# Twenty-six input projections as two-by-two block products with seven multiplications, in a hybrid decoder block

## The chip, the cores and the metric

The kernel runs on one core of one Trainium2 chip. The metric is the device time of one execution in microseconds (us). The engines are TensorE (PE in the rows), VectorE (DVE), ScalarE (ACT), GpSimd (POOL) and SyncE (SP), which here issues nearly all transfers.

## The reference

One decoder block, T = D = 1024, in float32:

```
h  = RMSNorm(x)
P  = h @ W_in        columns for retention, SSD, GLA heads and merge gates
a  = retention (4 heads), b = Mamba-2 SSD (16 heads, conv, 2 groups), c = GLA (4 heads)
x  = x + (sig(g_a)*a + sig(g_b)*b + sig(g_c)*c) @ W_out
x  = x + relu(RMSNorm(x) @ W_up)^2 @ W_down
out = final RMSNorm(x)
```

## The kernel before

Every large product is done in float32r parts: `split` takes an operand apart into hi (a cast on ACT) and lo (a subtraction on DVE), and `acc3` adds hi·hi, hi·lo and lo·hi in PSUM, three matmuls per 128 rows of depth. A weight comes by one SP transfer into `raw` and is split into `whi` and `wlo`.

W_in is cut into 34 sets of 256 columns. In channel form (`T_unit`) a set is four units of 24 matmuls of 128x512, with weights as the stationary operand and h as the moving one, so results have channels on the partitions. In token form (`tok_unit`) a unit is 24 matmuls of 128x256 (128x288 for the first set) for one block of 128 tokens. Two sets for retention's v and two for GLA's v were in token form. `x` came transposed from the host; 1/rms per token was applied to the products, by `rs_b` in DVE's reading of PSUM and by a scale in ACT's.

`stream` yields after each unit. `merge(main, nmain, mixer, nmix)` deals the steps of a mixer evenly over `nmain` units, in program order, which is the order on every engine's own queue. Retention and the first group of the SSD's projections ran together, then SSD group 0 with the projections of group 1, SSD group 1 with GLA's projections, and GLA (`gla_mixer`, 18 steps, two per chunk and two head pairs) with 28 of the 48 gate units. The other 20 were run by `gates_done`, called behind `load_o(0)`, which loads the first token half of the 16 mixer output tiles (`oraw`), scales them and splits them into `ohi` and `olo`. Then `branch_half(0)` multiplies these with `w_o`, and the output projection, the MLP and the last norm follow:

```
    merge(stream(g_jobs()), 32, ssd_mixer(1), 26)
...
    merge(itertools.islice(gates, 28), 28, gla_mixer(), 18)
...
    for _ in load_o(0, o):
        pass
    gates_done()
```

`finish_heads` squares each head's output on ACT (`hsq`), takes the power on POOL (`rs_r`), scales (`og`), transposes on TensorE, multiplies by the gate (`ot`) and stores. In GLA, ACT makes the decays (`kx`, `ge`), DVE the decayed operands (`kap`, `qbd`, `qg`) and the masked scores (`scm`).

Of the kernel before, what the change touches and what calls it, by code (L numbers as in the profile page):

```python
# [44 lines left out]

SET_V, SET_R, SET_S, SET_G, SET_M = 0, 2, 8, 18, 24
# [7 lines left out]
def _layout(inp):  # L54
    a = {}
    w_in = inp["w_in"][0].reshape(KD, P, -1)
    parts = [np.concatenate([w_in[:, :, lo:hi] for lo, hi in s], axis=2) for s in _in_sets()]
    a["w_vdg"] = parts[0].reshape(2, 4, P, 288).transpose(0, 2, 1, 3).reshape(2, P, 1152)
    w = np.stack(parts[1:]).reshape(len(parts) - 1, 2, 4, P, 256)
    a["w_in"] = w.transpose(0, 1, 3, 2, 4).reshape(len(parts) - 1, 2, P, 1024)  # L60
# [7 lines left out]
    a["x_t"] = inp["x"][0].reshape(NT, P, KD, P).transpose(0, 3, 2, 1).reshape(NT, P, D)  # L68
# [40 lines left out]
def block_kernel(ctx, tc, i, out):  # L109
# [4 lines left out]
    wp = ctx.enter_context(tc.tile_pool(name="wp", bufs=5))  # L114
# [13 lines left out]
    ident = load(const, "c_id", nc.gpsimd)  # L128
# [12 lines left out]
    def wslot(src, n=1024, cuts=1):  # L141
        raw = wp.tile([P, n], F32, name="raw", tag="raw", bufs=2)
        hi = wp.tile([P, n], F32R, name="whi", tag="whi")
        lo = wp.tile([P, n], F32R, name="wlo", tag="wlo")
        for q in range(cuts):
            sl = slice(q * n // cuts, (q + 1) * n // cuts)
            nc.sync.dma_start(out=raw[:, sl], in_=src[:, sl])
        for q in range(cuts):
            sl = slice(q * n // cuts, (q + 1) * n // cuts)
            split(hi[:, sl], lo[:, sl], raw[:, sl])  # L150
        return hi, lo

# [4 lines left out]
    def acc3(ps, pairs, first=True, last=True):  # L157
        n = 3 * len(pairs)
        j = 0
        for (ah, al), (bh, bl) in pairs:  # L160
            for l, r in ((ah, bh), (ah, bl), (al, bh)):
                PE.matmul(out=ps, lhsT=l, rhs=r, start=(first and j == 0), stop=(last and j == n - 1))  # L162
                j += 1

# [11 lines left out]
    gt_d = dram.tile([NT, P, 10, P], F32, name="gt_d")  # L176
    gv_d = [dram.tile([P, 512], F32, name=f"gv_{c}") for c in range(NT)]
# [5 lines left out]
    rs_d = dram.tile([NT, P], F32, name="rs_d")  # L183
# [3 lines left out]
    hhi = hp.tile([P, KD, T], F32R, name="hhi")  # L187
    hlo = hp.tile([P, KD, T], F32R, name="hlo")
    rs_b = hp.tile([P, T], F32, name="rs_b")
# [16 lines left out]
    wk = ast.enter_context(tc.tile_pool(name="wk", bufs=2))  # L206
    rst_ = ExitStack()
    rp = rst_.enter_context(tc.tile_pool(name="rp", bufs=1))
    cos = rp.tile([P, T], F32, name="cos")
    sin = rp.tile([P, T], F32, name="sin")  # L210
    pst = ExitStack()
    pro = pst.enter_context(tc.tile_pool(name="pro", bufs=4))

    def load_consts():
        for t, n in ((cos, "c_cos"), (sin, "c_sin"), (dm, "c_dm"), (qd, "c_qd"), (kd, "c_kd"), (tri, "c_tri"),
                     (msk, "c_msk"), (gw, "gate_w")):
            nc.sync.dma_start(out=t, in_=i[n])
        nc.sync.dma_start(out=rows, in_=i["rows"][0, :].partition_broadcast(P))

# [879 lines left out]
```

## Time and profile before

| | before |
|---|---|
| time, median of 3 runs (lowest to highest) | 1968.05 us (1965.75 to 1970.85) |
| the profiled execution: span, which is its own time | 1966.1 us |
| granted TensorE clock, mean | 0.998 |
| busy: TensorE, DVE, ACT, POOL | 1947.7, 953.5, 669.9, 212.4 us |
| largest wait of TensorE in the list | 2.9 us |

A matmul's row gives the time from its start to its end; successive ones overlap, so busy time is not a count of slots. "Idle before" is the time in which the engine had nothing running, with what ended it. One granted clock of 1.00 is 2.4 GHz.

### The profile page before, as it was taken

To read this page: it belongs to the slowest core of one execution; us is meant where nothing else is said; L and a number is where in the kernel's file an instruction comes from. 1 tells how busy PE (TensorE), PEld (TensorE's weight loads), DVE (VectorE), ACT (ScalarE), POOL (GpSimd) and SP (SyncE) were. 2 spreads that over 40 slices of the span, in tenths; PEclk is the share of its full clock that TensorE was granted. 3 is DMA by queue.
4 is the path that set the end of the run, shared out by engine and by line. 5 is a ranking of instruction groups with operands and counts; after the bars stand their busy time and mean duration, and the time that the engine had idled before them with its cause. 6 is when DMAs were issued, how large, how long until landed. Compare 5 with 4: busy or idle time off the path is not lost.

```text
span 1966.1 us, 24813 instructions
## 1 busy us (share of the span) xinstructions
PE 1947.7 (99%) x9745; PEld 1615.8 (82%) x9745; DVE 953.5 (48%) x1627; ACT 669.9 (34%) x1105; POOL 212.4 (11%) x229
## 2 busy tenths in 40 slices
PE   9999999999999999999999999999999999999998
PEld 8888878777778888888888989888888888888886
DVE  4534664895466355543257456543333333333334
ACT  5212363674244467633223223331221212121213
POOL 2211111221122110000021021000000000000003
PEclk9999999999999999999999999999999999999999
DMA  7534445554453434345366453111111111111112
GB/s 270 164 91 123 128 126 154 185 160 134 156 169 114 149 102 134 121 139 173 137 236 194 129 163 105 44 65 43 43 54 53 44 43 43 59 49 44 43 44 86
DMA packets 130276, 221.86 MB, mean 113 GB/s; under 512 B 10168, under 2 KB 76128, under 8 KB 130160
## 3 DMA queue, kind: packets, MB, share of 16 engines
q1 hardware_dynamic: 129696, 219.37, 35.3%
q8 instruction: 76, 1.25, 0.3%
q10 hardware_dynamic: 432, 0.85, 0.2%
q14 instruction: 40, 0.33, 0.0%
q0 software_dynamic: 32, 0.07, 0.0%
HBM read 168.79 MB, written 51.46 MB: 112 GB/s over the span
## 4 chain that ended last, share of the span: by engine, by line
PE 93%; DVE 3%; DMA 2%; ACT 1%; issue 1%; POOL 0%; SPq 0%; POOLq 0%; ACTq 0%; DVEq 0%
PE mm L162 86%; DVE cacc L353 1%; PE mx L607 1%; PE mx L729 1%; PE mx L612 1%; PE mx L616 0%; DMA oraw<-o 0%; DVE ab L592 0%; PE tp L952 0%; PE mx L494 0%; DVE wlo L155 0%; DMA raw<-w_in 0%; DMA xin<-st 0%; PE tp L476 0%; PE mx L748 0%
## 5 line engine op out<-in xcount | busy, mean ns | idle before, releaser
L162 PE MATMUL mm<-hhi,whi 128*128 128x512 f32 x1024 | 413.7, 404 | 0.0
L162 PE MATMUL mm<-hlo,whi 128*128 128x512 f32 x1024 | 406.9, 397 | 0.0
L162 PE MATMUL mm<-hhi,wlo 128*128 128x512 f32 x1024 | 405.8, 396 | 0.0
L154 ACT CAST whi<-raw 128x1024 fp32r<-128x1024 f32 (+1 forms) x186 | 193.4, 1041 | 585.9 <-PE mm L162 560.3
L155 DVE TENSOR_TENSOR wlo<-raw,whi 128x1024 fp32r<-128x1024 f32 (+1 forms) x186 | 244.5, 1314 | 183.1 <-ACT whi L154 182.7
L162 PEld LDWEIGHTS mm<-hhi,wlo 128*128 128x128 f32 x1024 | 192.0, 188 | 47.8 <-issue 1.7
L162 PEld LDWEIGHTS mm<-hhi,whi 128*128 128x128 f32 x1024 | 192.3, 188 | 46.2 <-issue 3.1
L162 PEld LDWEIGHTS mm<-hlo,whi 128*128 128x128 f32 x1024 | 192.4, 188 | 46.0 <-issue 3.1
L162 PE MATMUL mm<-h2hi,whi 128*128 128x512 f32 x512 | 202.6, 396 | 0.0
L162 PE MATMUL mm<-h2lo,whi 128*128 128x512 f32 x512 | 202.5, 396 | 0.0
L162 PE MATMUL mm<-h2hi,wlo 128*128 128x512 f32 x512 | 202.5, 396 | 0.0
L162 PE MATMUL mm<-whi,al 128*128 128x512 f32 x512 | 201.7, 394 | 0.0
L162 PE MATMUL mm<-wlo,ah 128*128 128x512 f32 x512 | 200.7, 392 | 0.0
L162 PE MATMUL mm<-whi,ah 128*128 128x512 f32 x512 | 198.8, 388 | 0.0
L1034 DVE TENSOR_TENSOR x<-mm,x 128x512 f32<-128x512 f32 x128 | 88.4, 691 | 179.3 <-PE mm L162 178.0
L1008 DVE TENSOR_TENSOR rl<-rl 128x512 f32<-128x512 f32 x64 | 44.2, 690 | 148.8 <-ACT rl L1007 148.8
L162 PEld LDWEIGHTS mm<-h2hi,wlo 128*128 128x128 f32 x512 | 96.1, 188 | 23.2
L162 PEld LDWEIGHTS mm<-h2hi,whi 128*128 128x128 f32 x512 | 96.1, 188 | 23.0
L162 PEld LDWEIGHTS mm<-h2lo,whi 128*128 128x128 f32 x512 | 96.1, 188 | 23.0
L162 PEld LDWEIGHTS mm<-wlo,ah 128*128 128x128 f32 x512 | 96.1, 188 | 22.6
L162 PEld LDWEIGHTS mm<-whi,ah 128*128 128x128 f32 x512 | 96.1, 188 | 21.6
L162 PEld LDWEIGHTS mm<-whi,al 128*128 128x128 f32 x512 | 96.3, 188 | 19.3
(238 smaller groups left out, 2899.7 us busy)
## 6 DMA issues: line engine op xcount, KB each, us to landing
raw<-w_in SPq DMA_DIRECT2D x70, 512.0 KB, 3.8
raw<-w_o SPq DMA_DIRECT2D x32, 512.0 KB, 4.0
raw<-w_up SPq DMA_DIRECT2D x32, 512.0 KB, 3.5
raw<-w_down SPq DMA_DIRECT2D x32, 512.0 KB, 4.3
gate<-gt SPq DMA_DIRECT2D x48, 256.0 KB, 2.1
gt<-gate SPq DMA_DIRECT2D x48, 256.0 KB, 3.0
xin<-st SPq DMA_DIRECT2D x16, 640.0 KB, 5.1
ab<-acs_d SPq DMA_DIRECT2D x16, 512.0 KB, 4.1
```

The costliest lines, as they stand in the source:

```text
L154: S.copy(out=dst_hi, in_=src)
L155: V.tensor_tensor(out=dst_lo, in0=src, in1=dst_hi.bitcast(F32), op=ALU.subtract)
L162: PE.matmul(out=ps, lhsT=l, rhs=r, start=(first and j == 0), stop=(last and j == n - 1))
L353: V.scalar_tensor_tensor(out=o, in0=raw[:, 1 + q:513 + q], scalar=cw_c[q][:, ct:ct + 1], in1=o, op0=ALU.mult, op1=ALU.add)
L607: PE.matmul(out=yd[f * SP:(f + 1) * SP, h // 2, :], lhsT=xs[:, h, :], rhs=ab[:, h, :], start=True, stop=True)
L612: PE.matmul(out=yo[:, k, :], lhsT=state[:, 2 * k:2 * k + 2, :].rearrange("p h d -> p (h d)"), rhs=xin[:, 5, :], start=True, stop=True)
L729: PE.matmul(out=sc[:, n * 64:(n + 1) * 64], lhsT=kap[q_][:, n, :], rhs=qbd[q_][:, n].rearrange("p h t -> p (h t)"), start=True, stop=True)
L1008: V.tensor_tensor(out=r, in0=r, in1=r, op=ALU.mult)
L1034: V.tensor_tensor(out=xs, in0=ps, in1=xs, op=ALU.add)
```

## The change

- Twenty-six sets (6 of retention, 10 of SSD, all 6 of GLA with its two v sets, 4 of the 12 gate sets) are two-by-two block products. h is cut into four blocks (by depth and by even and odd token blocks), the weights into four (by depth and by column half). Seven products of a sum of weights with a sum of h replace eight, each 12 matmuls of 128x512, so 84 for a set; the eight other gate sets ("plain") keep four units of 24.
- A set uses three PSUM banks. Two results need a product that stands in a bank with others: the bank is read after one product (`p1` by ACT, `us` by DVE), then accumulated into again. `prep` makes the weight sums for the next set on DVE, one step per product; `later` deals out the rotation and the convolution's taps, one per product, now over 1024 tokens.
- h is prepared up front: x is loaded by rows, normalised on ACT, transposed on TensorE (64 transposes of 128x128), multiplied by the norm's weight and split; four sums of its blocks go to `ht` (`x_comb`), and one block goes to DRAM (`b12_d`) and comes back when `ht` is free, for the plain sets. `rs_b` is gone.
- GLA's v now has channels on the partitions and is transposed on TensorE (32 transposes, 16 copies on ACT).
- Mixers: 17 block sets run with the decays alone, retention over the next nine, `log_decays` and both SSD groups over 24 plain units, GLA over the last eight. `gates_done` is gone.
- Smaller ones: `wp` has 4 buffers for weights instead of 5; `og` is scaled on ACT instead of DVE; in the SSD eight exponentials of 128x128 with a bias and one minimum replace eight DVE subtractions and one exponential.

```diff
-    wp = ctx.enter_context(tc.tile_pool(name="wp", bufs=5))
+    wp = ctx.enter_context(tc.tile_pool(name="wp", bufs=4))
...
-    def stream(jobs):
-        ahead = None
-        for n, (s, body) in enumerate(jobs):
-            ws = ahead if ahead is not None else in_set(s)
-            ahead = in_set(jobs[n + 1][0]) if n + 1 < len(jobs) else None
-            yield from body(ws)
...
+    def x_rows(c):
+        xr = pro.tile([P, D], F32, name="xr")
+        nc.sync.dma_start(out=xr, in_=i["x"][c])
+        sq = pro.tile([P, D], F32, name="xsq", bufs=1)
+        ss = wk.tile([P, 1], F32, name="ssx", tag="ss", bufs=6)
+        S.activation(out=sq, in_=xr, func=AF.Square, accum_out=ss)
+        v = wk.tile([P, 1], F32, name="vsx", tag="ss", bufs=6)
+        V.tensor_scalar(out=v, in0=ss, scalar1=1.0 / D, scalar2=EPS, op0=ALU.mult, op1=ALU.add)
+        r = wk.tile([P, 1], F32, name="rsx", tag="ss", bufs=6)
+        G.tensor_tensor(out=r, in0=v, in1=nhalf[:, 0:1], op=ALU.pow)
+        S.activation(out=xr, in_=xr, func=AF.Copy, scale=r)
+        return xr
...
+    def x_turn(xn, dst):
+        for q in range(2):
+            ps = ptp.tile([P, 4, P], F32, name="tp", tag="tp")
+            for k in range(4):
+                PE.transpose(out=ps[:, k], in_=xn[:, (4 * q + k) * P:(4 * q + k + 1) * P], identity=ident)
+            ks = slice(4 * q, 4 * q + 4)
+            V.tensor_tensor(out=dst[:, ks], in0=ps, in1=aw_c[:, ks].unsqueeze(2).broadcast_to([P, 4, P]), op=ALU.mult)
+
...
+    def x_chunk(c, xn):
+        j = c // 2
+        if c % 2 == 0:
+            e = pro.tile([P, KD, P], F32, name="xe", bufs=1)
+            x_turn(xn, e)
+            split(he[0][:, :, j], he[1][:, :, j], e)
+            even[j] = e
+            return [(he[0][:, k, j], he[1][:, k, j]) for k in range(KD)]
+        o = pro.tile([P, KD, P], F32, name="xo", bufs=1)
+        x_turn(xn, o)
+        ob = [pro.tile([P, 4, P], F32R, name=f"ob{q}", bufs=1) for q in range(2)]
+        split(ob[0], ob[1], o[:, 0:4])
+        split(hb22[0][:, :, j], hb22[1][:, :, j], o[:, 4:8])
+        for q in range(2):
+            nc.sync.dma_start(out=b12_d[q][:, :, j], in_=ob[q].bitcast(F32))
+        even[j] = (even[j], o)
+        return [(ob[0][:, k], ob[1][:, k]) for k in range(4)] + [(hb22[0][:, k, j], hb22[1][:, k, j]) for k in range(4)]
...
+        def two(sl, a, b):
+            hi, lo = wparts(None, raw[:, sl])
+            w[a], w[b] = ([t[:, o:o + 512] for t in (hi, lo)] for o in (0, 512))
+
+        if kind == "plain":
+            for n in range(2):
+                w[n] = wparts(None, raw[:, 1024 * n:1024 * n + 1024])
+                yield
+            return
+        two(slice(0, 1024), "a11", "a12")
+        yield
+        hi, lo = (wp.tile([P, 512], F32R, name="w22", tag=f"w22{q}", bufs=2) for q in range(2))
+        split(hi, lo, q3)
+        w["a22"] = (hi, lo)
+        V.tensor_tensor(out=q0, in0=q0, in1=q2, op=ALU.subtract)
+        yield
+        V.tensor_tensor(out=q2, in0=q2, in1=q3, op=ALU.add)
+        V.tensor_tensor(out=q3, in0=q3, in1=q0, op=ALU.subtract)
+        yield
+        two(slice(1024, 2048), "s1", "s2")
+        yield
+        V.tensor_tensor(out=q1, in0=q1, in1=q3, op=ALU.subtract)
+        yield
+        two(slice(0, 1024), "s3", "s4")
+        yield
...
+        def plus(ps, other):
+            t = up.tile([P, 512], F32, name="us", tag="us")
+            V.tensor_tensor(out=t, in0=ps, in1=other, op=ALU.add)
+            return t
+
+        px = bank()
+        prod(px, w["a11"], H["b11"], True)
+        p1 = up.tile([P, 512], F32, name="us", tag="us")
+        S.copy(out=p1, in_=px)
+        yield
+        py = bank()
+        prod(py, w["s2"], H["t2"], True)
+        u2 = plus(py, p1)
+        yield
+        prod(px, w["a12"], H["b21"], False)
+        emit(0, 0, px, None)
+        yield
+        prod(py, w["s1"], H["t1"], False)
+        u4 = plus(py, p1)
+        yield
+        pw = bank()
+        prod(pw, w["s3"], H["t3"], True)
+        emit(1, 1, pw, u4)
+        yield
+        prod(py, w["s4"], H["b22"], False)
+        emit(0, 1, py, p1)
+        yield
+        prod(pw, w["a22"], H["t4"], False)
+        emit(1, 0, pw, u2)
+        yield
...
+    def projections(jobs, raws, cur):
+        for n, (kind, s, emit) in enumerate(jobs):
+            nxt = {}
+            ahead = prep(jobs[n + 1][0], raws[n + 1], nxt) if n + 1 < len(jobs) else iter(())
+            for k, _ in enumerate(run_set(kind, cur, emit)):
+                if k == 0 and n + 2 < len(jobs):
+                    raws[n + 2] = fetch(jobs[n + 2][1])
+                next(ahead, None)
+                if later:
+                    later.pop(0)()
+                yield
+            for _ in ahead:
+                pass
+            cur = nxt
...
+            def tap(q):
+                V.scalar_tensor_tensor(out=o, in0=raw[:, 1 + q:T + 1 + q], scalar=cw_c[q][:, ct:ct + 1],
+                                       in1=o, op0=ALU.mult, op1=ALU.add)
+
+            def start():
+                S.activation(out=o, in_=raw[:, 4:T + 4], func=AF.Identity,
+                             scale=cw_c[3][:, ct:ct + 1], bias=cb_c[:, ct:ct + 1])
+                tap(0)
+
+            def end():
+                tap(2)
+                S.activation(out=o, in_=o, func=AF.Silu)
+                nc.sync.dma_start(out=st_d[g][:, :, slot, :].rearrange("c p t -> p c t"),
+                                  in_=o.rearrange("p (c t) -> p c t", t=P))
+            later.extend([start, lambda: tap(1), end])
...
         for h in range(2):
-            V.tensor_scalar(out=og[:, h * P:(h + 1) * P], in0=o_ps[:, h * P:(h + 1) * P],
-                            scalar1=r[:, h:h + 1], scalar2=None, op0=ALU.mult)
+            S.activation(out=og[:, h * P:(h + 1) * P], in_=o_ps[:, h * P:(h + 1) * P], func=AF.Copy,
+                         scale=r[:, h:h + 1])
...
                 nc.sync.dma_start(out=gin, in_=gt_d[c])
-                gv = gp.tile([P, 512], F32, name="gv", bufs=2)
-                nc.sync.dma_start(out=gv, in_=gv_d[c])
-                ins[c] = (gin, gv)
-            gin, gv = ins[c]
+                ins[c] = gin
+            gin = ins[c]
+            tv = ptp.tile([P, 512], F32, name="tp", tag="tp")
+            for h in range(2):
+                PE.transpose(out=tv[:, h * GV:(h + 1) * GV], in_=gin[:, 10 + 2 * q_ + h, :], identity=ident)
+            vp = gp.tile([P, 256], F32, name="gv", bufs=3)
+            S.copy(out=vp, in_=tv[:, 0:256])
             q, k, gg = gin[:, q_, :], gin[:, 2 + q_, :], gin[:, 4 + q_, :]
...
+    for n, (slot, func) in enumerate(((0, None), (2, None), (6, AF.Silu), (8, AF.Silu), (10, None), (12, None))):
+        jobs.append((SET_G + n, e_plain(gt_d, slot, func)))
+    jobs = [("block", *j) for j in jobs]
...
+    xn = {0: x_rows(0)}
+    w0 = [wslot(i["w_vdg"][q], 1152) for q in range(2)]
+    xn[1] = x_rows(1)
+    w1 = [wslot(i["w_v"][q]) for q in range(2)]
+    hc = {0: x_chunk(0, xn[0])}
+    xn[2] = x_rows(2)
+    raws, cur = {}, {}
+    for c in range(NT):
+        if c + 1 < NT:
+            hc[c + 1] = x_chunk(c + 1, xn.pop(c + 1))
+            if c + 3 < NT:
+                xn[c + 3] = x_rows(c + 3)
+            if c % 2 == 0:
+                x_comb(c // 2)
+        v_unit(c, hc[c], 0, w0)
+        if c < NT - 2:
+            v_unit(c, hc[c], 1, w1)
...
+    def run(n):
+        return itertools.islice(main, 7 * n)
+
+    for _ in run(3):
         pass
-    pst.close()
-    for _ in stream(r_jobs(0)):
+    merge(run(3), 21, decays(), 6)
...
+    for _ in run(11):
         pass
...
-    merge(stream(s_jobs(0)), 20, itertools.chain(ret_mixer(0), log_decays(), ret_mixer(1)), 42)
+    merge(run(9), 63, itertools.chain(ret_mixer(0), ret_mixer(1)), 38)
...
+    hb12p = hst.enter_context(tc.tile_pool(name="hb12p", bufs=1, side="right"))
+    H["b12"] = [hb12p.tile([P, 4, NJ, P], F32R, name=f"hb12{q}") for q in range(2)]
+    for q in range(2):
+        nc.sync.dma_start(out=H["b12"][q].bitcast(F32), in_=b12_d[q])
     sst = ExitStack()
...
-    merge(stream(s_jobs(1)), 20, ssd_mixer(0), 26)
-    merge(stream(g_jobs()), 32, ssd_mixer(1), 26)
...
+    merge(itertools.islice(main, 24), 24, itertools.chain(log_decays(ld), ssd_mixer(0), ssd_mixer(1)), 62)
...
-    merge(itertools.islice(gates, 28), 28, gla_mixer(), 18)
+    merge(itertools.islice(main, 8), 8, gla_mixer(), 18)
+    for _ in main:
+        pass
...
-    def gates_done():
-        for _ in gates:
-            pass
-        hst.close()
...
         pass
```

TensorE's order at the end of GLA and the start of the branch products. `og` are the last heads' outputs, `hhi` and `hlo` parts of h, `ohi` and `olo` parts of the mixer outputs, `whi` and `wlo` weights, `mm`, `mx` and `tp` banks of PSUM. Before:

```order
L162 MATMUL mm_7716<-hhi_150,wlo_7236 128x512
L476 MATMUL tp_7745<-k_c_id_77,og_7627 128x128 x2
L476 MATMUL tp_7751<-k_c_id_77,og_7713 128x128 x2
L162 MATMUL mm_7883<-hhi_150,whi_7541 128x512
...
L162 MATMUL mm_8470<-hhi_150,wlo_8263 128x512
L162 MATMUL mm_8528<-ohi_7769,whi_8515 128x512
L162 MATMUL mm_8528<-olo_7770,whi_8515 128x512
```

Between the last transposes of GLA's heads and the first branch matmul stand 480 matmuls of 20 gate units. The same place on TensorE now (`gst` is GLA's state, `scm` its scores):

```order
L852 MATMUL mx_8297<-gst11_7091,qg_8261 128x128
L853 MATMUL mx_8297<-gv_8240,scm1_7089 128x128
L575 MATMUL tp_8313<-k_c_id_77,og_8282 128x128 x2
L575 MATMUL tp_8319<-k_c_id_77,og_8310 128x128 x2
L159 MATMUL mm_8471<-ohi_8341,whi_8459 128x512
L159 MATMUL mm_8471<-olo_8342,whi_8459 128x512
L159 MATMUL mm_8471<-ohi_8341,wlo_8460 128x512
```

Nothing stands between them any more.

SP's queue there, before. `ot` are GLA's last outputs on their way to `o`, `rsy` the SSD's norms, `oraw` the tiles of `load_o(0)`:

```order
L479 DMA o_4_1_145<-ot_7748 128x2x128
L369 DMA gate_1_5_125<-gt_7741 128x512
L479 DMA o_4_1_145<-ot_7754 128x2x128
L147 DMA raw_8127<-w_in 128x1024
L867 DMA rsy_7763<-ys_d_111 128x512
L867 DMA rsy_7764<-ys_d_111 128x512
L871 DMA oraw_7767<-o_0_0_136 128x512
```

And now (`x2_1` to `x2_7` is the residual that the output projection adds to):

```order
L578 DMA o_4_1_137<-ot_8316 128x2x128
L578 DMA o_4_1_137<-ot_8322 128x2x128
L147 DMA raw_8613<-w_o 128x1024
L147 DMA raw_8619<-w_o 128x1024
L994 DMA rsy_8335<-ys_d_103 128x512
L994 DMA rsy_8336<-ys_d_103 128x512
L998 DMA oraw_8339<-o_0_0_128 128x512
L998 DMA oraw_8345<-o_0_0_128 128x512
L998 DMA oraw_8351<-o_1_0_130 128x512
L1091 DMA x2_1_8447<-x 128x1024
L1091 DMA x2_2_8448<-x 128x1024
L998 DMA oraw_8357<-o_1_0_130 128x512
```

The loads of x have moved from behind the gates to among the loads of o, seven of them in all; the `oraw` loads stay behind the last stores of `ot`.

DVE's order inside a convolution of retention's time, before: `craw` is a bank's reading, `cacc` a tap of 512 tokens, `rst` and `sm` belong to the retention mixer.

```order
L155 TENSOR_TENSOR wlo_2004<-raw_2002,whi_2003 128x1024
L347 TENSOR_TENSOR craw_1941<-mm_1916,rs_b_152 128x512
L155 TENSOR_TENSOR wlo_2308<-raw_2306,whi_2307 128x1024
L353 SCALAR_TENSOR_TENSOR cacc_1944<-craw_1941,k_cols_75,cacc_1944 128x512
L532 SCALAR_TENSOR_TENSOR rst_1959<-rst_1879,mx_1956 128x128
```

And the taps of a convolution now, which fall into the set behind it: `us` reads a bank that is used again (both times `mm_2023`), `raw` on both sides is a sum of the next set's weights, `wlo` a lo part of them.

```order
L446 SCALAR_TENSOR_TENSOR cacc_1997<-craw_1960,k_cols_75,cacc_1997 128x1024
L344 TENSOR_TENSOR us_2036<-mm_2023,us_2012 128x512
L312 TENSOR_TENSOR raw_1886<-raw_1886 128x512
L446 SCALAR_TENSOR_TENSOR cacc_1997<-craw_1960,k_cols_75,cacc_1997 128x1024
L313 TENSOR_TENSOR raw_1886<-raw_1886 128x512
L446 SCALAR_TENSOR_TENSOR cacc_1997<-craw_1960,k_cols_75,cacc_1997 128x1024
L152 TENSOR_TENSOR wlo_2078<-raw_1886,whi_2077 128x1024
L344 TENSOR_TENSOR us_2075<-mm_2023,us_2012 128x512
```

The readings of PSUM now stand between taps of double length and the sums of weights; the mixer is gone from here.

## Rows read from the trace of the kernel before

**Rows 1.** The page: busy time by engine, then the chain that ended last.

```profile
PE 1947.7 (99%) x9745; PEld 1615.8 (82%) x9745; DVE 953.5 (48%) x1627; ACT 669.9 (34%) x1105; POOL 212.4 (11%) x229
...
PE 93%; DVE 3%; DMA 2%; ACT 1%; issue 1%; POOL 0%; SPq 0%; POOLq 0%; ACTq 0%; DVEq 0%
```

**Rows 2.** TensorE's waits: total us, times, longest.

```profile
PE mm L162 <- ACT whi L154: 2.9, 2, 1.7
```

**Rows 3.** Windows: PE, PEld, DVE, ACT, POOL busy, then clock, DMA share, GB/s.

```profile
380.00:420.00 40.00, 39.89 (x227) 31.69 (x225) 39.50 (x77) 29.72 (x39) 11.61 (x12) 1.00 0.51 157
420.00:460.00 40.00, 38.72 (x211) 30.53 (x210) 40.00 (x77) 29.03 (x36) 11.49 (x11) 1.00 0.51 153
...
980.00:1020.00 40.00, 40.00 (x173) 32.25 (x172) 21.71 (x22) 10.48 (x12) 10.10 (x7) 1.00 0.75 258
```

**Rows 4.** The chain, 600 to 700 us: start, us, what.

```profile
614.30 0.50 PE tp L570 x4
...
637.81 22.82 PE mm L162 x192
...
660.74 22.39 PE mm L162 x96
```

**Rows 5.** The prologue: timeline of PE and ACT, groups, transfers.

```profile
9.04 0.38 PE L162 MATMUL mm<-whi,hhi 128*128 128x288 f32 x1
...
11.10 1.06 ACT L245 ACTIVATE xr<-xr 128x1024 f32<-128x1024 f32 x1 [1.48 <-DMA xr<-x]
...
L155 DVE TENSOR_TENSOR hlo<-xt,hhi 128x1024 fp32r<-128x1024 f32 x7 | 10.2, 1452 | 13.0 <-ACT hhi L154 13.0
...
L169 POOL TENSOR_TENSOR rs_r<-rs_v,nhalf 128x2 f32<-128x2 f32 x32 | 22.8, 712 | 167.5 <-DVE rs_v L167 167.5
...
xt<-x_t SPq DMA_DIRECT2D x7, 512.0 KB, 5.2
```

**Rows 6.** DVE's groups: busy us, mean ns, idle before.

```profile
L155 DVE TENSOR_TENSOR wlo<-raw,whi 128x1024 fp32r<-128x1024 f32 x182 | 241.4, 1327 | 182.7 <-ACT whi L154 182.3
...
L353 DVE SCALAR_TENSOR_TENSOR cacc<-craw,k_cols,cacc 128x512 f32<-128x512 f32 x72 | 58.1, 807 | 2.8 <-ACT cacc L350 2.5
...
L329 DVE TENSOR_TENSOR pl<-mm,rs_b 128x512 f32<-128x512 f32 x40 | 27.6, 690 | 85.2 <-PE mm L162 85.2
```

**Rows 7.** The window of GLA, line L162 alone: PE, PEld busy.

```profile
660.00:860.00 200.00, 171.14 (x691) 126.65 (x690) 1.00 0.34 111
```

**Rows 8.** ACT's timeline inside GLA, and one group of retention's scalings.

```profile
714.79 0.28 ACT L466 ACTIVATE hsq<-mx 128x128 f32<-128x128 f32 x1
...
715.58 1.28 ACT L720 ACT_TABLE_LOAD   x1
...
719.50 0.31 ACT L697 ACTIVATE ge<-ge 128x128 f32<-128x128 f32 x1 [2.42 <-DVE ge L695]
719.71 1.11 ACT L701 ACTIVATE kx<-gin,gsc 128x32 f32<-128x32 f32 x4
720.73 0.29 ACT L702 ACTIVATE ge<-gin 128x128 f32<-128x128 f32 x1
...
721.98 1.28 ACT L368 ACT_TABLE_LOAD   x1
723.28 0.72 ACT L368 ACTIVATE gt<-gt,k_cols 128x512 f32<-128x512 f32 x1
...
L509 ACT ACTIVATE ks<-tp,kd 128x128 f32<-128x128 f32 x28 | 8.9, 360 | 13.3 <-PE tp L506 8.3 <-issue 4.9
```

**Rows 9.** SP's timeline, then tile oraw from 856 to 902 us.

```profile
858.78 0.39 SPq L479 DMA_DIRECT2D o<-ot  x1
...
L871 SPq DMA_DIRECT2D oraw<-o x19: 319/320/432, 862.5 to 901.1; - x19
L880 ACT ACTIVATE ohi<-oraw,k_cols x8: 707/724/726, 868.4 to 899.6; 128x512 fp32r<-128x512 f32 x8
...
DMA to landing us min/median/max: 2.7/3.9/6.0
```

More of the change, by code (lines that the diff above doesn't have):

```diff
@@ L161, in acc3, with wcol @@
             for l, r in ((ah, bh), (ah, bl), (al, bh)):
-                PE.matmul(out=ps, lhsT=l, rhs=r, start=(first and j == 0), stop=(last and j == n - 1))
+                PE.matmul(out=ps, lhsT=l, rhs=r, start=(first and j == 0), stop=(last and j == n - 1),
+                          skip_group_check=open_)
                 j += 1
+    def wcol(ws, k, c0, n, width=256):
+        hi, lo = ws[k // 4]
+        o = (k % 4) * width + c0
+        return hi[:, o:o + n], lo[:, o:o + n]
     def rstd(pool, ss, n, width):
@@ L175, in block_kernel @@
     st_d = [dram.tile([NT, P, 10, P], F32, name=f"st_{g}") for g in range(SG)]
[L176 to L177 removed]
+    gt_d = dram.tile([NT, P, 14, P], F32, name="gt_d")
     acs_d = dram.tile([P, P], F32, name="acs_d")
@@ new lines, in block_kernel, with fetch, prep @@
+    later = []
+    def fetch(s):
+        raw = wp.tile([P, 2048], F32, name="raw", tag="raw", bufs=2)
+        nc.sync.dma_start(out=raw, in_=i["w_in"][s])
+        return raw
+    def prep(kind, raw, w):
+        q0, q1, q2, q3 = (raw[:, 512 * q:512 * q + 512] for q in range(4))
+        def two(sl, a, b):
[22 more added lines that the diff above has]
+        yield
@@ new lines, in prod, with run_set, bank @@
+    def prod(ps, a, b, first):
+        acc3(ps, [((a[0][:, k * P:(k + 1) * P], a[1][:, k * P:(k + 1) * P]), (b[0][:, k], b[1][:, k]))
+                  for k in range(4)], first=first, open_=not first)
+    def run_set(kind, w, emit):
+        def bank():
+            return pmm.tile([P, 512], F32, name="mm", tag="mm")
+        if kind == "plain":
+            for par in range(2):
+                bs = [H["b11"], H["b21"]] if par == 0 else [H["b12"], H["b22"]]
+                for n in range(2):
+                    ps = bank()
+                    hi, lo = w[n]
+                    acc3(ps, [((hi[:, k * P:(k + 1) * P], lo[:, k * P:(k + 1) * P]),
+                               (bs[k // 4][0][:, k % 4], bs[k // 4][1][:, k % 4])) for k in range(KD)])
+                    emit(n, par, ps, None)
+                    yield
+            return
+        def plus(ps, other):
[27 more added lines that the diff above has]
+        yield
@@ new lines, in block_kernel @@
+    for _ in prep(jobs[0][0], raws[0], cur):
+        pass
+    for c in (NT - 2, NT - 1):
+        v_unit(c, hc[c], 1, w1)
+    pst.close()
+    up = ast.enter_context(tc.tile_pool(name="up", bufs=4))
+    ac2 = ast.enter_context(tc.tile_pool(name="ac2", bufs=1))
+    tri = load(ac2, "c_tri")
+    nc.sync.dma_start(out=rows, in_=i["rows"][0, :].partition_broadcast(P))
+    rst_ = ExitStack()
+    rp = rst_.enter_context(tc.tile_pool(name="rp", bufs=1))
+    cos = load(rp, "c_cos")
+    sin = load(rp, "c_sin")
```

428 lines of the change are left out of this document (180 added, 248 removed).

## The prediction

> **What bounds the kernel now.** I read the page's first part and its chain of waits first: TensorE is busy for 1947.7 of 1966.1 us, and the chain that ended last lies on it for 93% [rows 1]. DVE with 953.5 us and ACT with 669.9 us have room on average. The list of TensorE's waits then names nothing large: its biggest entry is 2.9 us [rows 2]. So a matmul that disappears is worth its slot, and any hole that opens between matmuls is lost in full. An average says nothing of a stage, though, and this change presses three stages together. The windows show what a full neighbour costs: from 380 to 460 us DVE is busy 39.50 and 40.00 of 40 us, and TensorE still works 39.89 and 38.72 [rows 3]. A saturated DVE took 0.1 to 1.3 us per 40 us there, no more.
>
> **Matmuls removed.** The price is the slot from start to start, not the 0.4 us that a matmul's row gives as its duration, since those overlap. In the chain 96 matmuls of 128x512 take 22.39 us, so 0.2332 each, and 192 of 128x256 take 22.82 us, so 0.1189 each [rows 4]. Twenty-four sets in channel form go from 96 to 84 matmuls of 512, which is 288 fewer. Two GLA v sets go from 384 matmuls of 256 in all to 168 of 512. Net: 120 of 512 (28.0 us) and 384 of 256 (45.7 us), **-73.7 us**. The instruction order shows these counts, so they are not in doubt.
>
> The Trainium skill, "TensorE: Matmul & The Clock Gate", section "Back-to-back issue gap", lists 518 and 262 cycles for one isolated matmul of 512 and 256, which is an estimate of 0.216 and 0.109 us at 2.4 GHz. By it the saving would be 67.8 us instead of 73.7; the rows of this stream are longer, and I go by them.
>
> **GLA's v on TensorE.** Its channel form needs 32 transposes of 128x128; four such take 0.50 us in the chain [rows 4], which bounds it at 4.0, and inside a longer run of matmuls of this size they close up a little: **+3.5 us**.
>
> **The prologue.** Before, the first v matmul starts at 9.04 us, on a transposed x that needs only scaling and a split [rows 5]. Now x must be loaded (5.2 us as the transposed one had), squared, scaled by POOL's power (0.71), transposed, multiplied and split. ACT has eight pieces in order up to the first hi part of h: two squarings, two scalings, three casts of weights and h's own, by the squaring's row 1.06 each or 8.5 us [rows 5]. With the load that is 13.7, and the issue of the load, POOL and two hand-offs are 2 to 3 more by estimate: about 16.4 us, 7.4 later. The other seven blocks bring 56 transposes, 7 us by [rows 4], and lo parts of 1.45 us on DVE [rows 5]; but the v stretch before was itself waiting for weights and x, and much of this falls there. I take **+10 us**, between 5 (the earlier loads overlap the warm-up) and 16 (nothing hides).
>
> **Block sets.** Seven products of 12 matmuls are 2.8 us each. A bank that is read after one product is accumulated into again one product later, so DVE or ACT must have read it within 2.8 us. On DVE a set has three lo parts of 1024 (1.33 each), one of 512, four sums of weights, two of products and three emits at 0.69, and in a convolution six taps of 1024, twice the 0.81 of a 512 [rows 6]. That is 4.0 + 0.7 + 6.2 + 9.7 = 20.6 us against 19.6 us of matmuls; means count overlap of neighbours twice, so the true load is rather 17 to 18 us, near 90%. The retention mixers, which stood beside convolutions before, lie over nine sets with neither rotation nor convolution, where DVE has more room. Bounds: 26 sets are 510 us, by [rows 3] 1 to 17 us of loss; **+7 us**, since the taps are dealt out one per product.
>
> **SSD over 24 plain units**: the same row over some 190 us gives 0 to 6; the new emits need no DVE, but ACT gains eight small exponentials per chunk and a pair of table loads per gate. **+3 us**. The reload of b12 (2 MB, 8 us at the 258 GB/s of the densest window in [rows 3]) is covered by two units of 5.6 us that use only b11 and b21: 0; without that cover it would be the 8 us.
>
> **GLA over 8 units instead of 28.** From 660 to 860 us there were 691 main matmuls [rows 7], 161 us, so GLA's own cost about 39 us with all its waits. Between its first and last step there are now 168 main matmuls, 39.2 us; with 39 and 3.5 TensorE has 82 us of work there. ACT has: 32 head squares at 0.40 (two take 0.79), 52 kx at 0.26 (four take 1.02), some 38 ge at a like 0.23, 32 scalings that moved here from DVE (0.36 alone, 0.27 in a row), 30 copies of 128 or 256 columns at an estimated 0.25, 14 table loads at 1.30, 7 gates at 0.7 [rows 8], 4 casts of 1024 at 1 us (the squaring's width in [rows 5]): 79 us. Two engines, both full, that feed each other within every half chunk. What remains is how often they miss. By [rows 3] a nearly full pair loses 3%, 2.6 us of 82; at the other end each of 16 half chunks has a wait like the 2.42 us that ACT spends on DVE's ge [rows 8], 39 us. I take **+10 us** beyond the waits that were there before.
>
> The Trainium skill, "ScalarE: Activation LUTs", section "What ACT_TABLE_LOAD costs", gives 1283 ns for the load and a drain of some 1380 ns, about 2.66 us per switch. The trace agrees with the load alone: from its start to the next instruction 1.30 us pass [rows 8]. By the page the 14 loads would add an estimated 19 us.
>
> **The transition.** Behind GLA, 480 gate matmuls (112 us) used to stand, and load_o(0) ran under them. Now the first branch matmul is next, and it wants o. From the last GLA matmul to the store of its o: squares 0.8, power 0.7, scaling 0.7, four transposes 0.5, the multiplication under 0.7: some 3.3 us. From the issue of the last o store (858.78) to the first ohi (868.4) 9.6 us passed [rows 9]. The sixteen tiles then took until 899.6; three buffers with 3.9 us to land, 0.72 us for ohi [rows 9] and as much for DVE's part, some 5.4 us per round of three, give 29, and 9.4 MB (o, w_o, seven loads of x that SP now issues between them) at 258 GB/s [rows 3] give 36. I take 30. TensorE has 48 matmuls, 11.2 us, to do meanwhile: 3.3 + 9.6 + 30 - 11.2 = **+32 us**. Low end 18 (first tile after 6 us, the loads done in 20), high end 38.
>
> **Sum**: -73.7 + 3.5 + 10 + 7 + 3 + 10 + 32 = -8.2 us. Against the profiled 1966.1 that is 1957.9; the median shown, 1968.05, is 1.9 above that execution, so 1960 us.
>
> **Rivals.** *The saving shows.* If every hole takes its low end (prologue 5, blocks 1, SSD and GLA 0, transition 18, with 3.5), -46.2 us from 1968.05, 1922 us. For it: TensorE lost almost nothing beside a full DVE [rows 3]. Against it: the transition's loads cannot start before the last store on SP's queue. Chance 0.17.
> *GLA in lockstep, slower than before.* If the wait of 2.42 us recurs in each half chunk, GLA loses 39 instead of 10: 1989 us. It decides from 1.1 us per half chunk (18 us), where the gain is used up. For it: ACT's 79 against 82 us leaves no slack, and both run in a fixed order. Against: each first stage is issued a step ahead. Chance 0.18.
> *Banks read late.* Three re-accumulations a set, 78 in all; if each waits 0.5 us for DVE, 39 us instead of 7, 1992 us; it decides at 0.19 us each. For it: 90% load and pieces of 1.3 us in front of a read. Against: the 2.8 us of slack. Chance 0.13.
> *A switch of tables costs twice its load.* If ACT stood still for another 1.30 us at each of the 14 loads in GLA, 18 us that TensorE there has no slack for: 1978 us. The 1.30 us from a load to its follower [rows 8] speak against it: 0.02. The drain that the Trainium skill's page gives, above, would be such a stop.
>
> **How the numbers follow.** The forecast has 0.50, with a range of its own of 1938 to 1980 from the bounds above taken together. A measurement of this kernel tells 0.3% (6 us) from no change. Within the forecast I give 0.30 to faster by more, 0.12 to within, 0.08 to slower. The first rival adds 0.17 to faster; the others 0.03 to the same and 0.30 to slower: 0.47, 0.15, 0.38. For eight in ten the range reaches to 1928 and 1992.
>
> **What would show it.** Right: 2952 matmuls of 512 in the projection at 0.233; the first v matmul near 16 us; one hole of 25 to 35 us, in pieces, ahead of and between the first matmuls on ohi, ended by oraw's transfers; a GLA stretch of some 92 us with ACT over 80% busy. Wrong: waits of TensorE for us (L344) or p1 of more than 15 us in the block stretch; DVE full there while TensorE has holes; a GLA stretch over 105 us or under 85; a transition hidden because the o tiles come sooner than SP's order suggests.

## The result and the profile after

The change takes 1994.3 us (median of 4 runs, 1989.91 to 1995.31); the kernel before took 1967.2 us beside it. The ratio is 1.0132, with a 95% interval of 1.0117 to 1.0147: **slower by 1.3%**, where 1960 us were forecast in a range from 1928 to 1992. The profiled execution spans 1988.1 us, 22.0 more than that of before; its own time is 1989.91.

The page's first part and the chain after, answering to [rows 1]:

```profile
PE 1917.7 (96%) x9336; PEld 1566.0 (79%) x9336; DVE 1072.9 (54%) x1624; ACT 765.3 (38%) x1344; POOL 209.1 (11%) x223
...
PE 79%; DVE 6%; ACT 4%; DMA 4%; issue 3%; POOL 3%; SPq 0%; POOLq 0%; DVEq 0%; ACTq 0%
```

TensorE is busy for 30 us less and idle for 52 us more. The list of its waits, which had 2.9 us on top before [rows 2], says behind what (total us, times, longest):

```profile
PE tp L740 <- POOL ysq L736: 19.5, 15, 2.4
PE mm L159 <- ACT ohi L1007: 13.1, 2, 11.1
PE mm L159 <- DVE us L344: 5.6, 4, 2.3
...
PE mx L709 <- DVE ab L697: 3.8, 1, 3.8
PE mm L159 <- DVE olo L152: 2.9, 4, 1.3
PE mx L597 <- DMA rin<-rt: 2.9, 5, 1.0
```

The first line was not in the forecast at all. L740 is the SSD's statistic: `ysq`, a chunk's squared output summed over its four parts by POOL, is multiplied with a column of ones. The windows show where the time lies (columns as in [rows 3]):

```profile
80.00:160.00 80.00, 76.56 (x321) 60.86 (x320) 67.86 (x88) 22.60 (x28) 17.87 (x11) 0.98 0.32 99
...
240.00:320.00 80.00, 80.00 (x345) 64.26 (x344) 56.28 (x69) 33.39 (x38) 0.00 (x0) 1.00 0.31 95
...
640.00:680.00 40.00, 35.73 (x134) 25.04 (x133) 20.71 (x37) 32.77 (x43) 2.08 (x2) 0.83 0.50 156
...
720.00:760.00 40.00, 33.29 (x207) 25.25 (x203) 29.45 (x38) 28.29 (x57) 17.18 (x14) 1.00 0.56 180
...
960.00:1000.00 40.00, 22.98 (x47) 12.49 (x48) 19.42 (x28) 11.26 (x18) 1.73 (x1) 0.57 0.82 275
```

From 240 to 320 us, in convolution sets, TensorE is full: the block products as such cost nothing but their matmuls. Before that (rotation sets), the SSD (from 645 us) and the transition (960 to 1000) leave holes. In the SSD no engine is full: in the window of 40 us from 720 us DVE has 29.45, ACT 28.29, POOL 17.18. The chain of waits through one chunk shows why TensorE waits all the same (start, us, what):

```profile
743.09 1.02 PE mx L709 x16
744.12 1.10 PE mx L714 x8
...
745.24 0.70 DVE eb L729
...
746.58 0.68 DVE sst L725
747.26 0.61 DVE y L731
...
747.89 0.64 ACT ysq L734
...
748.60 1.51 POOL ysq L735
...
750.19 1.33 POOL ysq L736
...
751.56 0.38 PE tp L740 x2
751.94 0.57 PE mm L159 x2
752.51 1.02 PE mx L709 x16
```

It is a ring. A chunk's products (L709, L714) go to DVE, ACT and POOL, POOL's sum to the statistic, and the next chunk's products stand right behind that statistic on TensorE. This turn takes 9.4 us, whatever else TensorE could do, and it is one of the shorter ones: from the first product with `ab` (673.8 us) to the last (841.0) sixteen chunks take 167.2 us, 11.1 a turn. The list above has the wait for the statistic in 15 of the 16 chunks.

### The profile page after: what moved, and what is told of

It reads as the page before. It is cut to its first block, busy times and chain, and to the rows that moved or that the text cites. A ratio compares the mean times of both kernels' runs of the same rounds, so it can differ in the third digit from the quotient of the medians.

```text
span 1988.1 us, 24150 instructions
## 1 busy us (share of the span) xinstructions
PE 1917.7 (96%) x9336; PEld 1566.0 (79%) x9336; DVE 1072.9 (54%) x1624; ACT 765.3 (38%) x1344; POOL 209.1 (11%) x223
## 4 chain that ended last, share of the span: by engine, by line
PE 79%; DVE 6%; ACT 4%; DMA 4%; issue 3%; POOL 3%; SPq 0%; POOLq 0%; DVEq 0%; ACTq 0%
PE mm L159 73%; DMA oraw<-o 2%; POOL ysq L735 1%; DMA rin<-rt 1%; DVE rb L419 1%; ACT ab L696 1%; PE mx L709 1%; DVE wlo L152 1%; PE mx L714 1%; DMA hb<-b 1%; PE mx L597 0%; POOL ysq L736 0%; PE mx L834 0%; ACT whi L151 0%; PE tp L1074 0%
## 5 line engine op out<-in xcount | busy, mean ns | idle before, releaser
L151 ACT CAST whi<-raw 128x1024 fp32r<-128x1024 f32 (+1 forms) x210 | 220.3, 1051 | 618.9 <-PE mm L159 570.0
L152 DVE TENSOR_TENSOR wlo<-raw,whi 128x1024 fp32r<-128x1024 f32 (+1 forms) x210 | 275.2, 1311 | 155.7 <-ACT whi L151 154.9
L159 PE MATMUL mm<-he,whi 128*128 128x512 f32 x672 | 216.2, 401 | 0.0
L159 PE MATMUL mm<-ht,whi 128*128 128x512 f32 x624 | 198.9, 400 | 5.6 <-DVE us L344 5.6
L159 PE MATMUL mm<-hb,whi 128*128 128x512 f32 x464 | 153.0, 406 | 0.5 <-DMA hb<-b 0.5
L159 PEld LDWEIGHTS mm<-he,whi 128*128 128x128 f32 x672 | 125.2, 189 | 28.4 <-issue 0.5
L159 PEld LDWEIGHTS mm<-ht,whi 128*128 128x128 f32 x624 | 116.2, 189 | 34.2 <-DVE us L344 7.3
L159 PE MATMUL mm<-he,wlo 128*128 128x512 f32 x336 | 134.6, 401 | 0.0
L159 PE MATMUL mm<-ht,wlo 128*128 128x512 f32 x312 | 123.9, 397 | 0.0
L159 PE MATMUL mm<-ohi,whi 128*128 128x512 f32 x256 | 104.8, 412 | 15.3 <-ACT ohi L1007 13.1
```

The lines of the kernel that those rows point to most:

```text
L151: S.copy(out=dst_hi, in_=src)
L152: V.tensor_tensor(out=dst_lo, in0=src, in1=dst_hi.bitcast(F32), op=ALU.subtract)
```

## The experiments

Ratios are to the kernel before, run beside; the change itself has 1.0132.

| run | median us | ratio, 95% interval |
|---|---|---|
| e1_stats_at_end | 1984.97 | 1.0086, 1.0070 to 1.0102 |
| e2_exp_gates | 1970.06 | 1.0013, 1.0003 to 1.0022 |
| e3_eight_oraw | 1981.11 | 1.0066, 1.0051 to 1.0081 |
| e4_residual_later | 1989.86 | 1.0109, 1.0092 to 1.0126 |
| e5_tanh_gates | 1972.02 | 1.0020, 1.0011 to 1.0029 |
| e6_tanh_stats_end | 1974.69 | 1.0027, 1.0016 to 1.0039 |
| e7_tanh_loads | 1953.45 | 0.9920, 0.9903 to 0.9936 |
| e8_tanh_keep_four | 1950.15 | 0.9902, 0.9888 to 0.9917 |
| e9_tanh_all | 1938.47 | 0.9841, 0.9828 to 0.9855 |
| e10_one_exp | 1977.78 | 1.0037, 1.0023 to 1.0051 |
| e11_og_on_dve | 1991.95 | 1.0117, 1.0099 to 1.0134 |
| e12_rotation_apart | 1996.38 | 1.0134, 1.0120 to 1.0149 |
| e13_tanh_one_exp | 1969.59 | 1.0014, 1.0004 to 1.0024 |
| e14_all_one_exp | 1937.59 | 0.9846, 0.9829 to 0.9863 |
| e15_plain_turn | 1986.39 | 1.0095, 1.0077 to 1.0113 |

### The SSD: the statistic, or ACT?

**e1**, the statistics in one row at the end:

```diff
-            def stat():
-                ps = ptp.tile([P, 512], F32, name="tp", tag="tp")
-                PE.matmul(out=ps[:, 0:1], lhsT=sq[:, 0], rhs=ones[:, 0:1], start=True, stop=True)
...
     def ssd_rows():
+        ps = ptp.tile([P, 512], F32, name="tp", tag="tp")
+        for k in range(2 * NT):
+            PE.matmul(out=ps[:, k:k + 1], lhsT=ysum[:, k], rhs=ones[:, 0:1], start=True, stop=True)
```

> The statistics of the SSD's chunks (a matmul of ysq with ones) are kept until both groups are done, in a tile of their own, and made there in one row; nothing else is changed. Theory A (the SSD lost its time because the scheduler put each chunk's statistic right ahead of the next chunk's first products on TensorE, behind a chain over DVE, ACT and POOL that takes 10 to 12 us a chunk): TensorE's waits for ysq, 21 us, go, the SSD's stretch from 662 to 847 us shrinks by 18 to 26 us, and the time is 1968 to 1976 us. Theory B (ACT, busy for about 155 of 186 us there with 42 table loads and 128 small exponentials, is the bound): the wait moves to other products, and no more than 6 us are gained, 1988 to 1994 us.

It gained 9 us (0.0046 of 1967), between the two theories. The stretch from the first to the last product with `ab` shrank by 20 us, from 167.2 to 147.3, but other waits took over in its list, for `ab` itself and later for GLA's `og`:

```profile
PE mx L709 <- DVE ab L697: 8.2, 6, 4.4
PE tp L575 <- ACT og L569: 6.5, 6, 1.9
...
PE tp L755 <- POOL rs_r L172: 2.5, 1, 2.5
```

So in the SSD's own stretch theory A holds, with ACT's load unchanged: a turn fell from 11.1 to 9.8 us. But only 9 of the 20 us arrived at the end. The new row of statistics waits for POOL (L755), the granted clock is 0.50 from 850 to 855 us behind that, and GLA waits longer for `og` (2.3 us in the change); the runs do not say how the 11 us divide among these.

**e2**, the gates' function:

```diff
-            S.activation(out=r, in_=ps if other is None else r, func=AF.Sigmoid,
+            S.activation(out=r, in_=ps if other is None else r, func=AF.Exp,
```

> The gates take Exp in place of Sigmoid, so the gate function is another one than the reference's; the work is the same, but ACT need not change its table between gates and exponentials. Theory B (ACT's table loads bound the SSD and GLA): 15 to 30 us less, 1964 to 1979 us. Theory A (the chain of the statistic): ACT's part in that chain is one square, and only a few of the loads stand in front of it; the loads removed give 2 to 8 us, in GLA above all, 1986 to 1992 us.

It gained 23 us, as theory B said. **e5** does it and keeps the reference's gates:

```diff
-            S.activation(out=r, in_=ps if other is None else r, func=AF.Sigmoid,
-                         bias=mb_c[:, 8 * b + d:8 * b + d + 1])
+            S.activation(out=r, in_=ps if other is None else r, func=AF.Tanh, scale=0.5,
+                         bias=mbh[:, 8 * b + d:8 * b + d + 1])
...
-                V.tensor_tensor(out=gt, in0=ps, in1=gt, op=ALU.mult)
+                V.scalar_tensor_tensor(out=gt, in0=gt, scalar=1.0, in1=ps, op0=ALU.add, op1=ALU.mult)
...
-            split(m[0], m[1], acc)
+            S.activation(out=m[0], in_=acc, func=AF.Copy, scale=0.5)
+            V.scalar_tensor_tensor(out=m[1], in0=acc, scalar=0.5, in1=m[0].bitcast(F32), op0=ALU.mult, op1=ALU.subtract)
```

> The gates as (1 + tanh(z/2))/2: ACT makes tanh, whose table it shares with Exp, and the 1 and the half go into the branch's multiplication and split on DVE and ACT. The result is the reference's. If the table loads themselves cost what e2 gained, 1966 to 1974 us. If e2 gained it from anything else that its other function brought, 1985 to 1994 us.

22 us, so e2's gain came with the loads and not with its other function. ACT's groups from 680 to 760 us, first of the change, then of e5 (busy us, mean ns, idle before):

```profile
L696 ACT ACTIVATE ab<-ab,nacs 128x128 f32<-128x128 f32 x64 | 19.6, 390 | 10.2 <-DVE ab L694 10.2
L468 ACT ACT_TABLE_LOAD x7 | 9.0, 1283 | 0.1
L693 ACT ACTIVATE eb<-ab 64x512 f32<-64x512 f32 x13 | 8.2, 627 | 0.1
L693 ACT ACT_TABLE_LOAD x6 | 7.7, 1283 | 0.1
...
L696 ACT ACT_TABLE_LOAD x1 | 1.3, 1283 | 0.0
```

```profile
L698 ACT ACTIVATE ab<-ab,nacs 128x128 f32<-128x128 f32 x72 | 22.2, 389 | 14.6 <-DVE ab L696 14.5
L695 ACT ACTIVATE eb<-ab 64x512 f32<-64x512 f32 x14 | 8.7, 625 | 2.6 <-DMA ab<-acs_d 2.6
```

In the same 80 us fourteen loads, 18 us, are gone, and nine chunks' worth of small exponentials fit in place of eight. The Trainium skill, "ScalarE: Activation LUTs", section "Table sets: the hidden batching unit", lists tanh in the set of exp; e5's rows agree, there is no load between gates and exponentials.

Why then did the statistic's place cost in the change and not before? Its program order is the same, behind the next chunk's products. The order on TensorE, which a scheduler makes, is not. In the change's trace each chunk's statistic runs ahead of the next chunk's products; with e5 it runs behind them from the second chunk on, as before the change. One chunk of each, first of the change, then of e5:

```profile
751.56 0.38 PE L740 MATMUL tp<-ones,ysq 128*128 128x1 f32 x2 [1.53 <-POOL ysq L736]
...
752.44 1.09 PE L709 MATMUL mx<-ab,xs 128*64 128x128 f32 x16
```

```profile
725.75 1.09 PE L711 MATMUL mx<-ab,xs 128*64 128x128 f32 x16
...
728.63 0.28 PE L742 MATMUL tp<-ones,ysq 128*128 128x1 f32 x2
```

So e5 changed two things, ACT's load and the place of the statistic; e2 did the same.

**e6** puts e5 and e1 together:

> e5 and e1 together. Theory A (the place of the statistic costs on its own, 17 of the SSD's 30 us): 8 to 15 us below e5, 1955 to 1962 us. Theory C (the statistic came early because ACT's load stretched each chunk; in e2, without table loads, its place was already behind the next chunk's first products, so there is nothing left to move): within 4 us of e5, 1966 to 1974 us.

No gain over e5 (1.0027 against 1.0020, intervals that overlap): theory C. With ACT relieved there is nothing left to win from the statistic. Against e1, which has the loads and no statistic in the ring either, e6 is 0.0059 lower, 12 us. By this estimate some 12 of e5's 22 us are the loads by themselves, and the other 10 hang on the statistic's place.

**e10** relieves ACT in another way, by undoing the other edit in the SSD:

```diff
-            V.tensor_tensor(out=ab, in0=ab, in1=acs[:, c, hs].unsqueeze(2).broadcast_to([P, R, P]), op=ALU.min)
             for h in range(R):
-                S.activation(out=ab[:, h, :], in_=ab[:, h, :], func=AF.Exp, bias=nacs[:, c, g * R + h:g * R + h + 1])
+                V.tensor_scalar(out=ab[:, h, :], in0=ab[:, h, :], scalar1=acs[:, c, g * R + h:g * R + h + 1],
+                                scalar2=0.0, op0=ALU.subtract, op1=ALU.min)
+            S.activation(out=ab, in_=ab, func=AF.Exp)
```

> The change with the SSD's exponentials as before: eight subtractions on DVE and one Exp of 1024 columns a chunk, in place of one minimum on DVE and eight Exp of 128 on ACT. ACT loses some 22 us of work in the SSD's 167 us, DVE gains 9 to 25. If it is ACT's load as a whole that bounds that stretch, 6 to 12 us are gained, 1982 to 1988 us. If the table loads alone matter, because they fall between gates and exponentials, or if DVE's part of the chain is as tight, 1991 to 2003 us.

19 us by the ratio (0.0095), more than either expectation, though DVE has more to do. **e13** joins it with e5:

> e5 and e10 together: no table loads between gates and exponentials, and one Exp a chunk. If table loads and small exponentials fill the same place, ACT's part in a chunk, so that either removal already takes the wait away, the sum saturates: 1963 to 1970 us. If they cost in different places, they add up: 1950 to 1958 us.

1.0014 against e5's 1.0020: it saturates. Either cure suffices. Both relieve ACT's part of a chunk, and with both the statistic moves behind the next products (of the 14 chunks that have a next one in their group, in all with e13 and in 11 with e10). That ACT's part is the one place where both cost fits this; the runs do not part it from the order.

### The transition

**e3** gives `oraw` more buffers; **e4** lets a DVE copy of the first merged tile into each of the residual's tiles hold back their loads:

```diff
-            raw = bp.tile([P, 512], F32, name="oraw", tag="oraw", bufs=3)
+            raw = bp.tile([P, 512], F32, name="oraw", tag="oraw", bufs=8)
```

```diff
+            if h == 0 and d == 0:
+                for c in range(NT):
+                    V.tensor_copy(out=x2[c][:, 0:1], in_=m[0][:, 0:1].bitcast(F32))
```

> load_o has eight buffers for the tiles of o instead of three. If the 32 us of the transition are rounds of three tiles that each wait for landing, ACT and DVE (latency), the loads run ahead and 8 to 14 us are gained, 1980 to 1986 us. If it is the rate of the DMA engines (304 to 340 GB/s in windows of 5 us there), the gain is under 4 us.

> The loads of the residual x wait for the first merged tile (a tiny copy into each of their tiles holds them back), so they no longer stand among the loads of o. If the rate of the DMA engines sets the transition, 3.7 MB less in it give 8 to 12 us, 1982 to 1986 us. If the rounds of three buffers set it, the loads of o come a little sooner each and 2 to 5 us are gained, 1989 to 1992 us.

13 us and about 4.5 us. The rounds of buffers are shown; the residual's share is not clear of the noise by itself, since e4's interval reaches that of the change. **e7**, both on top of e5:

> e5 with eight buffers for the tiles of o and the residual's loads held back. If the transition's two parts are independent of the mixers, e3's 13 and e4's 4 us come on top of e5: 1949 to 1956 us, faster than the kernel before. If buffers and residual relieve the same wait, only the larger counts: 1955 to 1960 us.

0.9920, 20 us below e5, where e3 and e4 have 17.5 together: the parts add up. **e8** brings back some cover, on e5:

```diff
-    merge(itertools.islice(main, 8), 8, gla_mixer(), 18)
-    for _ in main:
-        pass
+    merge(itertools.islice(main, 4), 4, gla_mixer(), 18)
...
     for _ in load_o(0, o):
         pass
+    for _ in main:
+        pass
```

> e5 with four of GLA's eight gate units kept back and run behind the start of load_o(0), 22 us of matmuls under the transition. If GLA is bound by TensorE and ACT together and ACT's 18 us of table loads are gone, GLA shrinks nearly by the 22 us that it gives away and the hole of 31 us shrinks by 18 to 22: 1950 to 1956 us. If GLA's chain of steps needs the units as cover, it keeps its length and the sum does not move: 1966 to 1974 us.

22 us below e5, the whole worth of the four units. GLA's products with `kap`, first and last start, in e5 and e8:

```profile
L836 PE MATMUL mx<-qbd,kap x128: 221/275/276, 850.5 to 934.9; 128*128 128x64 f32 x128
```

```profile
L836 PE MATMUL mx<-qbd,kap x128: 219/275/323, 848.7 to 914.0; 128*128 128x64 f32 x128
```

GLA got 19 us shorter with half its units: it had no use for them as cover. **e9** has all of e7 and e8, **e14** e10 too:

> e8 with eight buffers for the tiles of o and the residual's loads held back. In e8 some 14 us of waits of TensorE for ohi and olo are left. If those are rounds of buffers and transfers, as e3, e4 and e7 would have it, 6 to 12 us go: 1938 to 1945 us. If the four units kept back already hide what can be hidden, 1948 to 1952 us.

> e9 and e10 together, the version that should be best. By saturation, 1932 to 1938 us; by addition, 1918 to 1925 us.

0.9841 and 0.9846: the version that keeps the block products, with tanh gates, four units behind GLA, eight buffers and the residual held back, is 1.5 to 1.6% faster than the kernel before. In e9 the last product of GLA stands at 919 us and the first branch matmul at 940; this is TensorE's only wait from 915 to 1000 us, and the window behind it is full:

```profile
PE tp L577 <- ACT og L571: 0.7, 1, 0.7
...
960.00:1000.00 40.00, 40.00 (x173) 32.20 (x173) 23.80 (x27) 10.61 (x12) 10.32 (x8) 1.00 0.94 334
```

### GLA and the rotation sets

**e11** puts `og` back on DVE:

```diff
-            S.activation(out=og[:, h * P:(h + 1) * P], in_=o_ps[:, h * P:(h + 1) * P], func=AF.Copy,
-                         scale=r[:, h:h + 1])
+            V.tensor_scalar(out=og[:, h * P:(h + 1) * P], in0=o_ps[:, h * P:(h + 1) * P],
+                            scalar1=r[:, h:h + 1], scalar2=None, op0=ALU.mult)
```

> The change with the heads' scaling back on DVE. If GLA's 12 us of waits come from ACT being full, 32 scalings less on it give 3 to 6 us, 1988 to 1991 us. If they come from the order of the steps (e2 and e5 took 21 us of ACT's work out of GLA and left its 86 us as they were), nothing changes: 1992 to 1997 us.

Unclear: 3 us lower, with intervals that overlap. **e12** swaps retention's plain set with its second rotation set:

```diff
-        jobs += [(n, e_rot(p, 0)), (n + 1, e_rot(p, 2)), (n + 2, e_plain(rt_d[p], 4, AF.Silu))]
+        jobs += [(n, e_rot(p, 0)), (n + 2, e_plain(rt_d[p], 4, AF.Silu)), (n + 1, e_rot(p, 2))]
```

> The change with retention's plain set between its two sets with rotation, in both pairs of heads, so that DVE's densest sets no longer follow each other. If DVE's backlog in two rotation sets in a row makes the late readings of banks (7 us of waits in front of products with ht, all before 190 us), 3 to 7 us are gained, 1987 to 1991 us. If each rotation set makes its own, nothing changes: 1993 to 1996 us.

Nothing changed beyond the noise, so a backlog that one set leaves to the next is not what costs here. **e15** takes DVE work out of the turn itself (one product of 128 rows with the sine, so the rotation is another one):

```diff
-                for q in range(2):
-                    src, to = slice(64 * q, 64 * q + 64), slice(64 - 64 * q, 128 - 64 * q)
-                    V.tensor_tensor(out=b3[to], in0=r3[src], in1=halves(sin)[par][src], op=ALU.mult)
+                V.tensor_tensor(out=b3, in0=r3, in1=halves(sin)[par], op=ALU.mult)
```

> The change with one product of 128 rows with the sine in place of two of 64 that swap the halves, so retention's rotation is left wrong and DVE has 0.69 us less in each of 16 turns; everything else stays. If DVE's load in the four rotation sets makes the banks' late readings there, the 5.6 us of waits for us before 190 us halve or go and 2 to 6 us are gained, 1988 to 1992 us. If they come from somewhere else in front of the readings, such as the lo parts of 1.3 us, they stay: 1993 to 1996 us.

7 us by the ratio (0.0037); no wait for `us` is left in its list, and the window from 80 us is full, with DVE at 66.29 of 80:

```profile
80.00:160.00 80.00, 79.91 (x343) 63.91 (x342) 66.29 (x89) 22.57 (x28) 16.55 (x12) 1.00 0.35 106
```

## Why the prediction was wrong

**The step that failed is "SSD over 24 plain units", +3 us.** It took the price of a full neighbour from [rows 3], at most 1.3 us per 40 us, and got 0 to 6. What it was worth: removing ACT's table loads alone gave 22 us (e5), undoing the small exponentials alone 19 (e10), both together 23 (e13), each with the statistic's place changed as well. The prediction had named both, "eight small exponentials per chunk and a pair of table loads per gate", and had not added them up against the time that a chunk now has. In [rows 3] DVE was full, but a chunk had 13.3 us there (six in 80 us by `ab`'s groups). Now sixteen chunks pass in 167.2 us, 11.1 a turn, and without ACT's loads in 138.7 (e5, 669.6 to 808.3), 9.2 a turn. The ring through TensorE, DVE, ACT and POOL, 9.4 us in the turn shown above, sets the pace although DVE is busy for 120.12 and ACT for 122.41 of the 167 us from 674 to 841, some three quarters. A busy share cannot show that. Nor did the prediction look where the statistic stood on TensorE now; the order would have shown it, and the front part's remark that program order is the order on every engine is not quite so.

The other steps held, roughly, but for the block sets (below). *Matmuls removed*: a piece of the chain from 189.91 us has 984 matmuls in 229.60 us, 0.2333 each, the price used. *Prologue* (+10): the first product of 512 columns starts at 71.8 us against 63.5, +8.3, and the first v matmul at 15.1 against an expected 16.4. *Block sets* (+7): TensorE lost next to nothing in the convolution sets, where I feared it, and some 7 us in the four rotation sets (e15). *Transition* (+32): between the last matmul of GLA at 957 us and full pace at 1004.5 us, 47.5 us, TensorE made 54 branch matmuls, worth 12.6 us at 0.2333; 35 us lost. *GLA* (+10, a stretch of 92 us): its products with `kap` lie between 871.5 and 955.1 us, the whole stretch up to the last matmul 85.6 us, some 4 over the 82 of TensorE's work. So GLA was overcharged by 6, and its rival, GLA in lockstep, was wrong, with its reason too: taking 18 us of table loads from ACT there did not shorten it (e5). Nor did a load cost twice its length: from one to its follower 1.29 us pass in GLA (953.89 to 955.18).
*The b12 reload* (0, "covered") was covered but for TensorE's 0.5 us wait for `hb`. The chain has its 9.96 us of transfer from 633.33, but TensorE worked through the rest of it. Its granted clock was 0.60 from 645 to 650 us, where small matmuls of the log decays also lie; the two are not told apart here.

The rival that came nearest in size, banks read late, was the wrong place: its waits made 5.6 us. No rival had the SSD. The sum of what is measured (-73.7, 3.5, 8.3, 7, 22 to 25 for the SSD, 4, 35) is 6 to 9 us, while the span grew by 22.0. So some 13 to 16 us are missing.

Where they went can be estimated from the traces. Give each matmul the start-to-start time that is usual for its kind in them, and call lost what a stretch takes beyond that: 52 us before and 137 in the change. The rotation sets lost 10, the convolution sets 3, the stretch beside retention 12, and the SSD from its log decays on 52; before, the same work lost 28. That is 48 us more, where the sum above has 29 to 32 for them, so about what is missing lies there. By it the SSD's term was some 27 us instead of 3, and the block sets' term, with retention, some 21 instead of 7; with another choice of the usual time they come to 24 and 18. Of the 12 us beside retention 4.7 are idle time (77.24, 78.84 and 79.23 of 80 us busy from 400 to 640 us). In the SSD the stretch from 640 to 680 us has 4.3 us idle and a granted clock of 0.83, up to 7 us of slots stretched that no row of waits shows. What makes the rest of retention's loss stays open, as does which of ACT's instructions in the SSD's ring counts most.

## What to carry to other kernels

When mixers are packed closer, compare the time that one step now has with the length of the chain that one step runs through, engine by engine, table loads included; a share of busy time bounds neither. Look at where a scheduler puts a small instruction that waits on a long chain, since everything behind it on its engine waits too. And keep independent matmuls for the place where one phase's last store is the next phase's first load: four units there gave back their full 22 us, and GLA did without them.

## What was not expected of the hardware

In the transition TensorE was idle for 11.12 us ahead of the first branch matmul, and what followed ran at half pace. The timeline:

```profile
972.16 0.77 PE L159 MATMUL mm<-ohi,whi 128*128 128x512 f32 x1 [11.12 <-ACT ohi L1007]
...
973.99 0.63 PE L159 MATMUL mm<-ohi,whi 128*128 128x512 f32 x1
974.41 0.63 PE L159 MATMUL mm<-olo,whi 128*128 128x512 f32 x1
974.84 0.63 PE L159 MATMUL mm<-ohi,wlo 128*128 128x512 f32 x1
```

They start 0.43 us apart instead of 0.233. The granted clock is 1.00 from 957 to 960 us and 0.50, the level of 1.2 GHz, from 960 to 975; before it fell TensorE had been idle for 2.28 us and had begun the four transposes of 959.64. So a hole costs more than its own length. The prediction let the branch's 48 matmuls run at full pace meanwhile. And POOL's sum of 256 columns (`ysq`, L735 now) took 1365 ns on average in the SSD from 630 to 850 us, where it had taken 871 ns before (380 to 660 us); it lies in the ring.
